# Loads of y inside the last gate, statistics through ScalarE's DMA queue, and joint weights two steps after their loads

## The chip, the cores and the metric

One NeuronCore of a Trainium2 chip. The metric is the device time of one execution in microseconds (us). The kernel before was timed in three runs: median 1971.28 us, from 1967.11 to 1976.27.

## The reference

A trunk of two layers over one sequence of 1024 tokens, width 1024, in float32. In each layer a token mixer's output is gated by a SiLU and projected:

```python
# layer 0: dilated attention, three groups (window, dilation) = (128,1), (512,4), (2048,16), 16 heads each
outs, lses = per group: softmax attention over the window, and its log-denominator
alpha = jax.nn.softmax(jnp.stack(lses, axis=0), axis=0)        # joint weights over the three groups
o = jnp.sum(alpha[..., None] * jnp.stack(outs, axis=0), axis=0)
y = o.reshape(B, S, DIL_WIDTH) * jax.nn.silu(gate)
return y @ w_out
# layer 1: differential attention, 8 heads of two softmaxes, per-head RMSNorm, the same gate and projection
```

Around each mixer stand an RMSNorm before and one after, and the residual.

## The kernel before

**Numbers.** Matmuls run on float32 values split into a high and a low part; a projection is three products (high×high, high×low, low×high). `XH` and `XL`, both resident, are the two parts of the layer's transposed input, 8 tiles of 128 rows called kt 0 to 7. Later the same memory takes the two parts of y, the gated mixer output.

**Layer 0.** Work goes by pairs of heads (`pr` 0 to 7), in a pair by group (`g` 0 to 2), in a unit `(pr, g)` by its two heads `h`. A head has four steps (c = 0 to 3). The main loop (L789 to L828) runs at step i the scores of step i, the transposes of step i − 3 and the products of step i − 5 (`LAG_T`, `LAG_P`). In a step the scores go to PSUM (L603), VectorE masks them and takes the maximum (L610), ScalarE takes the exponential (L613), TensorE transposes (L626), ScalarE and VectorE copy and split the result (`pp`, L630 and L122), TensorE multiplies by v (L653, L665) and ScalarE, VectorE and POOL add up `u` (L671 to L686).

**Filler.** Between these TensorE pieces stand matmuls of the projections: for layer 0 `pqk` (L276: q and k of later units, which are rotated by VectorE and POOL in L248 to L253, stored to `qk_d` by L261 and loaded per head as `qh`, `ql`, `ka` by L268 and L270), then the last gate block (`pg`, also L276, from `late_gates` L311 and `gate_units` L280), then the early part of the output projection (`pe`, L444, in `out_early` L425). The last gate walks kt 0 and 1, then kt 2, 3 up to 7, each for both halves of the tokens, so that a kt's rows of `XH` and `XL` are free once its products are done. After it ScalarE loads the table for the silu (L320), applies it, and loads the exponential's table back.

**Output.** `out_early` loads y of kt 0 to 3 from `y_d` into `XH` and `XL` (`load_y`, L400 to L402, two DMAs of 512 KB per kt), multiplies them with `w_out` (`ow`, `wh`, `wl`, split by L184 and L122 from `raw`, loaded by L421), and stores partial sums (L449, L452). The loads of kt 4 to 6 and the rest follow. Layer 1 uses the same functions; its scores are L951.

**Statistics.** Each head keeps its row maxima and denominators in `st`. `put_stats` (L688) stores them to `st_d`: for g = 0 TensorE transposes them (`tps`, L692), VectorE copies that to `sr` (L694) and four DMAs follow (L699); g = 1 and 2 store `st` directly, four DMAs each (L702, L706). All are of 4 KB. After g = 2 `joint` (L708) loads them as `js` (two DMAs, L712), works out the joint weights on VectorE (L718 to L728) with one exponential on ScalarE (L722), and stores them to `wt_d` (L730). `combine` (L733), a generator of steps run two and four steps later, loads the weights broadcast (`wb`, L753) and the gate (`sil_in`, L763), multiplies on POOL (L759 to L764) and stores y (`y_d`, L384).

**Order.** TensorE's order is set by hand. The order on the other engines and on SP, which issues every DMA, comes from a list scheduler that starts from the order in which the program traces its calls. A DMA, whichever engine issues it, carries one of eight completion semaphores (DMAHW0 to DMAHW7) in turn over the whole program, and the engine that issues it waits until the DMA that carried that semaphore eight places earlier has landed. Each engine runs its instructions in order.

Of the kernel before, what the change touches and what calls it, by code (L numbers as in the profile page):

```python
# [18 lines left out]
P = 128  # L19
# [18 lines left out]
EARLY = 4  # L38
# [54 lines left out]
def trunk(ctx: ExitStack, tc: tile.TileContext, a: dict, out: bass.AP):  # L93
    nc = tc.nc
# [26 lines left out]
    def low(eng, o, full, hi):  # L121
        return eng.tensor_tensor(o, full, hi.bitcast(F32), ALU.subtract)  # L122
# [42 lines left out]
    def ts(j, w=P):  # L165
        return slice(j * w, (j + 1) * w)
# [51 lines left out]
    latest = {}  # L218
# [54 lines left out]
    def project(o, wh, wl, tok, kts=range(KT)):  # L273
        for kt in kts:
            for k, (l, r_) in enumerate(((wh, XH), (wh, XL), (wl, XH))):
                nc.tensor.matmul(o, lhsT=l[:, kt, :], rhs=r_[:, kt, tok],  # L276
                                 start=kt == 0 and k == 0, stop=kt == KT - 1 and k == 2)
                yield 512

    def gate_units(pool, layer, w, fs, eng=None, prepare=None):  # L280

        for f in fs:
            wh, wl = w_tiles([P, KT, P])
            split(wh, wl, load(w[f], [P, KT, P]), eng)
            if prepare and f == fs[-1]:
                prepare()
                banks = [ps.tile([P, 512], F32, tag="pj", name="pg") for _ in range(2)]
                for kts in ((0, 1), *((kt,) for kt in range(2, KT))):
                    for c in range(2):
                        yield from project(banks[c], wh, wl, ts(c, 512), kts)  # L290
                for c in range(2):
                    yield f, c, banks[c]
                return
            for c in range(2):
                o = ps.tile([P, 512], F32, tag="pj", name="pg")
                yield from project(o, wh, wl, ts(c, 512))
                yield f, c, o
# [70 lines left out]
    stored = set()  # L368
# [31 lines left out]
    def load_y(layer, kt):  # L400
        for e, x in enumerate((XH, XL)):
            nc.sync.dma_start(x[:, kt, :].bitcast(F32), y_d[layer][kt, e])  # L402
# [22 lines left out]
    def out_early(pool, layer, w, ws):  # L425

        ws[EARLY - 1] = out_weights(pool, w, EARLY - 1)
        for kt in range(EARLY):
            while (layer, kt) not in stored:
                yield None  # L430
            load_y(layer, kt)
        for n in range(NB):
            if n == NB - HELD:
                while ("heads", layer) not in written:
                    yield None
                for kt in range(EARLY, KT - 1):
                    ws[kt] = out_weights(pool, w, kt)
            parts = []
            for c in range(2):
                bank = ps.tile([P, 512], F32, tag="pj", name="pe")  # L440
                for kt in range(EARLY):
                    wh, wl = ws[kt]
                    for k, (l, r_) in enumerate(((XH, wh), (XH, wl), (XL, wh))):
                        nc.tensor.matmul(  # L444
                            bank, lhsT=l[:, kt, ts(n)], rhs=r_[:, ts(c, 512)],
                            start=kt == 0 and k == 0, stop=kt == EARLY - 1 and k == 2)
                        yield 512
                t = pool.tile([P, 512], F32, tag="t", name="part", bufs=3 - layer)
                nc.scalar.copy(t, bank)  # L449
                parts.append(t)  # L450
            for o, t in zip(partial(n), parts):
                nc.sync.dma_start(o, quarters(t))  # L452
        ws[KT - 1] = out_weights(pool, w, KT - 1)
        banks = ws["banks"] = out_banks(0)
        for kt in range(EARLY, KT - 1):
            while (layer, kt) not in stored:
                yield None
            load_y(layer, kt)
            yield from out_block(0, banks, kt, *ws[kt], kt == EARLY, False)
# [96 lines left out]
    with tc.tile_pool(name="l0", bufs=2) as lp:  # L556
# [4 lines left out]
        class Head:  # L561
# [56 lines left out]
            def transposes(self, c):  # L618

                tp = ps.tile([P, 512], F32, tag="pt", name="tp")  # L620
                n = 0
                for kb in (2 * c, 2 * c + 1):
                    for b in (kb, kb + 1):
                        if (b, kb) in self.pb:
                            self.pt[kb, b] = n
                            nc.tensor.transpose(out=tp[:, ts(n)], in_=self.pb.pop((b, kb)), identity=ident)  # L626
                            n += 1
                w_ = n * P
                pp = lp.tile([P, 2, 512], F32R, tag="pp", name="pp")
                nc.scalar.copy(pp[:, 0, :w_], tp[:, :w_])  # L630
                low(nc.vector, pp[:, 1, :w_], tp[:, :w_], pp[:, 0, :w_])
                self.parts[c] = pp

            def product(self, c):
# [53 lines left out]
        def put_stats(pr, g, st):  # L688

            if g == 0:  # L690
                tp = ps.tile([P, 512], F32, tag="pt", name="tps")
                nc.tensor.transpose(out=tp[:32, :P], in_=st.rearrange("p h e b -> p (h e b)"), identity=ident)  # L692
                sr = lp.tile([32, P], F32, tag="sr", name="sr", bufs=1)
                nc.vector.tensor_copy(sr, tp[:32, :P])  # L694
            for h in range(2):
                for e in range(2):
                    row = st_d[2 * pr + h, g, e]
                    if g == 0:
                        nc.sync.dma_start(  # L699
                            row.rearrange("(b q) -> b q", b=8), sr[16 * h + 8 * e : 16 * h + 8 * e + 8, :])  # L700
                    elif g == 1:
                        nc.sync.dma_start(  # L702
                            row.rearrange("(f q r) -> q f r", f=2, r=4),
                            st[:, h, e, :].rearrange("p (f r) -> p f r", f=2))
                    else:
                        nc.sync.dma_start(row.rearrange("(q r) -> q r", r=8), st[:, h, e, :])  # L706

        def joint(pr):  # L708

            s = lp.tile([P, NG, 2, 16], F32, tag="js", name="js", bufs=1)  # L710
            for h in range(2):
                nc.sync.dma_start(  # L712
                    s[64 * h : 64 * h + 64],
                    st_d[2 * pr + h].rearrange("g e (p i) -> p g e i", i=16))
            m, den = s[:, :, 0, :], s[:, :, 1, :]
            mx = lp.tile([P, 16], F32, tag="jm", name="jm", bufs=1)
            e = lp.tile([P, NG, 16], F32, tag="je", name="je", bufs=1)
            nc.vector.tensor_tensor(mx, m[:, 0, :], m[:, 1, :], ALU.min)  # L718
            nc.vector.tensor_tensor(mx, mx, m[:, 2, :], ALU.min)
            for g in range(NG):  # L720
                nc.vector.tensor_sub(e[:, g, :], mx, m[:, g, :])
            nc.scalar.activation(e, e, AF.Exp)  # L722
            nc.vector.tensor_mul(den, den, e)
            nc.vector.tensor_add(mx, den[:, 0, :], den[:, 1, :])
            nc.vector.tensor_add(mx, mx, den[:, 2, :])
            nc.vector.reciprocal(mx, mx)
            for g in range(NG):
                nc.vector.tensor_mul(e[:, g, :], e[:, g, :], mx)  # L728
            for h in range(2):
                nc.sync.dma_start(  # L730
                    wt_d[2 * pr + h].rearrange("g (p i) -> p g i", i=16), e[64 * h : 64 * h + 64])
# [51 lines left out]
        us, stats, due = {}, {}, {}  # L783
# [5 lines left out]
        for i in range(nst + LAG_P):  # L789
            if i < nst:  # L790
                hd, c = heads[i // 4], i % 4
                if c == 0 and hd.h == 0:
                    stats[hd.pr, hd.g] = lp.tile([P, 2, 2, NB], F32, tag="st", name="st")
                    us[hd.pr, hd.g] = lp.tile([P, T], F32, tag="u", name="u", bufs=4)
                if c == 0:
                    hd.st, hd.u = stats[hd.pr, hd.g][:, hd.h], us[hd.pr, hd.g]
                if c == 1 and i // 4 + 1 < len(heads):
                    nxt = heads[i // 4 + 1]
                    fill.until(NG * nxt.pr + nxt.g)
                    nxt.load()  # L800
                hd.scores(c)
                if i == nst - 1:
                    written.add(("heads", 0))
                fill.at((3 * i + 1) / 24)
                if c == 3 and hd.h == 1 and hd.g == NG - 1:
                    put_stats(hd.pr, hd.g, stats.pop((hd.pr, hd.g)))
                    joint(hd.pr)
            if 0 <= i - LAG_T < nst:
                hd, c = heads[(i - LAG_T) // 4], (i - LAG_T) % 4
                hd.transposes(c)  # L810
# [322 lines left out]
```

## Time and profile before

| what | value |
|---|---|
| timed runs, median of 3 | 1971.28 us |
| profiled execution | 1973.98 us |
| its span, first to last instruction | 1972.1 us |
| mean granted TensorE clock | 0.986 |
| ScalarE, VectorE, POOL busy | 45%, 50%, 40% of the span |
| DMA moved | 397.90 MB, mean 202 GB/s |

The rest of the numbers stand beside the argument below. In the profile PE is TensorE's matmuls, PEld its weight loads, DVE VectorE, ACT ScalarE, POOL GpSimd, and SPq the issue of DMAs on SP. A row of the waits reads: who waited, at which line, for what, us in total, times, longest. A row of the chain of waits or of the timeline begins with the start and the length in us; `out<-in` are the program's names; in brackets stands the idle time ahead and what ended it. In a row of stretches, the stretch is followed by busy times of PE, PEld, DVE, ACT and POOL with their instruction counts, then the granted clock, the DMA engines' busy share and GB/s.

### The profile page before, as it was taken

To read this page: it belongs to the slowest core of one execution; us is meant where nothing else is said; L and a number is where in the kernel's file an instruction comes from. 1 tells how busy PE (TensorE), PEld (TensorE's weight loads), DVE (VectorE), ACT (ScalarE), POOL (GpSimd) and SP (SyncE) were. 2 spreads that over 40 slices of the span, in tenths; PEclk is the share of its full clock that TensorE was granted. 3 is DMA by queue.
4 is the path that set the end of the run, shared out by engine and by line. 5 is a ranking of instruction groups with operands and counts; after the bars stand their busy time and mean duration, and the time that the engine had idled before them with its cause. 6 is when DMAs were issued, how large, how long until landed. Compare 5 with 4: busy or idle time off the path is not lost.

```text
span 1972.1 us, 29075 instructions
## 1 busy us (share of the span) xinstructions
PE 1888.0 (96%) x10008; PEld 1587.9 (81%) x10008; DVE 985.4 (50%) x2618; ACT 885.3 (45%) x2043; POOL 784.2 (40%) x553
## 2 busy tenths in 40 slices
PE   7999999999999999999999878999989899999897
PEld 5788888888888888888888767788878798897786
DVE  5311221135555555555555635550177877778626
ACT  4212112135656565656565555342244455446532
POOL 0000001154585867676776532320742435423011
PEclk9999999999999999999999979999999999999899
DMA  6424344277798989898989798442644565556643
GB/s 225 161 91 133 117 145 155 91 233 219 213 294 239 296 242 283 249 280 259 271 267 267 237 329 217 165 167 87 207 155 132 181 213 182 166 182 196 239 158 128
DMA packets 217539, 397.90 MB, mean 202 GB/s; under 512 B 40880, under 2 KB 123312, under 8 KB 217392
## 3 DMA queue, kind: packets, MB, share of 16 engines
q1 hardware_dynamic: 217392, 396.04, 63.8%
q8 instruction: 80, 1.31, 0.3%
q14 instruction: 67, 0.55, 0.1%
HBM read 254.87 MB, written 132.71 MB: 197 GB/s over the span
## 4 chain that ended last, share of the span: by engine, by line
PE 74%; DMA 10%; DVE 7%; POOL 3%; ACT 3%; issue 2%; SPq 1%; POOLq 0%; ACTq 0%; DVEq 0%
PE pqk L276 29%; PE pv L213 17%; PE pg L276 8%; PE po L391 4%; PE sc L603 3%; PE sc L951 3%; PE pe L444 2%; PE tp L626 2%; PE up L653 2%; PE ob L1004 2%; DMA ql<-qk_d 2%; DMA raw<-in_dil_w_out_dram 1%; DMA qk_d<-r 1%; PE tp L984 1%; DMA wb<-wt_d 1%
## 5 line engine op out<-in xcount | busy, mean ns | idle before, releaser
L276 PE MATMUL pqk<-XL,wh 128*128 128x512 f32 x1024 | 418.7, 409 | 0.0
L276 PE MATMUL pqk<-XH,wh 128*128 128x512 f32 x1024 | 408.3, 399 | 1.7 <-DVE t L252 1.7
L276 PE MATMUL pqk<-XH,wl 128*128 128x512 f32 x1024 | 408.6, 399 | 0.0
L122 POOL TENSOR_TENSOR wl<-raw,wh 128x1024 fp32r<-128x1024 f32 x59 | 141.7, 2401 | 512.3 <-ACT wh L184 509.7
L613 ACT ACTIVATE pm<-pm,st 128x128 f32<-128x128 f32 (+1 forms) x384 | 170.4, 444 | 149.5 <-DVE st L610 148.6
L276 PEld LDWEIGHTS pqk<-XH,wh 128*128 128x128 f32 x1024 | 193.2, 189 | 31.5 <-DVE t L252 3.5
L276 PEld LDWEIGHTS pqk<-XH,wl 128*128 128x128 f32 x1024 | 193.5, 189 | 26.9
L276 PEld LDWEIGHTS pqk<-XL,wh 128*128 128x128 f32 x1024 | 193.1, 189 | 26.9
L122 DVE TENSOR_TENSOR pp<-tp,pp 128x512 fp32r<-128x512 f32 (+2 forms) x192 | 104.3, 543 | 132.5 <-ACT pp L630 131.7
L184 ACT CAST wh<-raw 128x1024 fp32r<-128x1024 f32 x96 | 100.6, 1047 | 144.4 <-PE pqk L276 65.8
L961 ACT ACTIVATE pm<-pm,mx 128x256 f32<-128x256 f32 (+7 forms) x128 | 99.4, 777 | 126.8 <-DVE mx L960 61.1
L213 PE MATMUL pv<-vwh,XH 128*128 128x512 f32 x384 | 153.0, 398 | 2.0 <-ACT XH L158 2.0
L213 PE MATMUL pv<-vwh,XL 128*128 128x512 f32 x384 | 153.0, 398 | 2.0 <-DVE XL L122 1.3
L213 PE MATMUL pv<-vwl,XH 128*128 128x512 f32 x384 | 152.2, 396 | 0.0
L122 DVE TENSOR_TENSOR vs<-pv,vs 128x512 fp32r<-128x512 f32 x64 | 44.2, 690 | 202.2 <-ACT vs L518 194.7
L610 DVE CUSTOM_DVE_ANT_0 pm<-sc,masks 128x128 f32<-128x128 f32 (+1 forms) x384 | 119.1, 345 | 27.2 <-PE sc L603 26.5
L630 ACT CAST pp<-tp 128x512 fp32r<-128x512 f32 (+2 forms) x192 | 89.6, 467 | 80.7 <-PE up L653 62.2
L954 DVE CUSTOM_DVE_ANT_0 pm<-sc,md 128x512 f32<-128x512 f32 (+3 forms) x192 | 102.6, 551 | 38.0 <-PE sc L951 35.5
L122 DVE TENSOR_TENSOR wl<-raw,wh 128x1024 fp32r<-128x1024 f32 x37 | 49.1, 1326 | 137.0 <-ACT wh L184 136.7
L251 POOL TENSOR_TENSOR r<-t 128x512 f32<-128x512 f32 x64 | 84.4, 1319 | 80.2 <-DVE t L250 79.1
L518 ACT CAST vs<-pv 128x512 fp32r<-128x512 f32 x48 | 28.1, 586 | 186.8 <-PE pv L213 186.8
L276 PE MATMUL pg<-XH,wh 128*128 128x512 f32 x256 | 103.1, 403 | 5.0 <-DVE t L252 5.0
(514 smaller groups left out, 4435.4 us busy)
## 6 DMA issues: line engine op xcount, KB each, us to landing
qk_d<-rh SPq DMA_DIRECT2D x64, 512.0 KB
qk_d<-r SPq DMA_DIRECT2D x64, 512.0 KB
qh<-qk_d SPq DMA_DIRECT2D x128, 256.0 KB
ql<-qk_d SPq DMA_DIRECT2D x128, 256.0 KB
ka<-qk_d SPq DMA_DIRECT2D x64, 512.0 KB
v_d<-vs SPq DMA_DIRECT2D x48, 512.0 KB
raw<-in_dil_qk_dram SPq DMA_DIRECT2D x48, 512.0 KB
vt<-v_d SPq DMA_DIRECT2D x48, 512.0 KB
```

What stands on the lines that cost most here:

```text
L122: return eng.tensor_tensor(o, full, hi.bitcast(F32), ALU.subtract)
L184: nc.scalar.copy(wh, raw)
L213: nc.tensor.matmul(o, lhsT=l, rhs=r_, start=first and k == 0, stop=last and k == 3 * KT - 1, skip_group_check=True)
L251: nc.gpsimd.tensor_sub(put(r[0]), nat(t1), nat(t2))
L276: nc.tensor.matmul(o, lhsT=l[:, kt, :], rhs=r_[:, kt, tok], start=kt == 0 and k == 0, stop=kt == KT - 1 and k == 2)
L391: nc.tensor.matmul(banks[c], lhsT=l[:, kt, ts(n)], rhs=r_[:, ts(c, 512)], start=first and k == 0, stop=last and k == 2,)
L603: nc.tensor.matmul(sc[:, cols], lhsT=q[:, ts(b)], rhs=kv, start=k == 0, stop=k == 1)
L610: nc.vector.tensor_tensor_reduce(pm[:, cols], sc[:, cols], m[:, m.shape[1] - w_ :], 1.0, 3.0e38, ALU.add, ALU.min, st[:, 0, j : j + 1])
L613: nc.scalar.activation(pm[:, cols], pm[:, cols], AF.Exp, bias=st[:, 0, j : j + 1], scale=-1.0, accum_out=st[:, 1, j : j + 1])
L630: nc.scalar.copy(pp[:, 0, :w_], tp[:, :w_])
L954: nc.vector.tensor_tensor_reduce(pm[:, k0:k1], sc[:, :w_], m_, 1.0, 3.0e38, ALU.add, ALU.min, mx[:, j : j + 1])
L961: nc.scalar.activation(pm[:, :wq], pm[:, :wq], AF.Exp, bias=mx[:, 0:1], scale=-1.0, accum_out=den)
```

## The change

Three edits. (1) y's loads of kt 0 to 3 are traced inside the last gate, as soon as a kt's gate products are traced, and no longer in `out_early`, where they came after the whole gate. (2) Statistics are stored through ScalarE's queue, 96 DMAs of 4 KB, and the copy to `sr` goes from VectorE to ScalarE, eight times. (3) `joint` stops after its two loads; its arithmetic and its stores run two steps later (one for the last pair), placed behind the latest `low` of a `pp`.

```diff
@@ gate_units
                 for kts in ((0, 1), *((kt,) for kt in range(2, KT))):
                     for c in range(2):
                         yield from project(banks[c], wh, wl, ts(c, 512), kts)
+                    for kt in kts:
+                        if kt < EARLY:
+                            load_y(layer, kt)
@@ out_early
         ws[EARLY - 1] = out_weights(pool, w, EARLY - 1)
-        for kt in range(EARLY):
-            while (layer, kt) not in stored:
-                yield None
-            load_y(layer, kt)
@@ Head.transposes
-                low(nc.vector, pp[:, 1, :w_], tp[:, :w_], pp[:, 0, :w_])
+                latest["low"] = low(nc.vector, pp[:, 1, :w_], tp[:, :w_], pp[:, 0, :w_]).ins
@@ put_stats
-                nc.vector.tensor_copy(sr, tp[:32, :P])
+                nc.scalar.copy(sr, tp[:32, :P])
...
-                        nc.sync.dma_start(
+                        nc.scalar.dma_start(
                             row.rearrange("(b q) -> b q", b=8), sr[16 * h + 8 * e : 16 * h + 8 * e + 8, :])
...
-                        nc.sync.dma_start(
+                        nc.scalar.dma_start(
...
-                        nc.sync.dma_start(row.rearrange("(q r) -> q r", r=8), st[:, h, e, :])
+                        nc.scalar.dma_start(row.rearrange("(q r) -> q r", r=8), st[:, h, e, :])
@@ joint
                     st_d[2 * pr + h].rearrange("g e (p i) -> p g e i", i=16))
+            yield
+
+            with tc.issue_after(latest["low"]):
+                weigh(pr, s)
+
+        def weigh(pr, s):
@@ main loop
-                    joint(hd.pr)
+                    due[i + (2 if hd.pr < 7 else 1)] = job = joint(hd.pr)
+                    next(job)
```

TensorE's order is the same in both. On SP at layer 0's last gate, from the second store of the last unit's rotated half (`qk_d<-r`) on, before:

```order
L261 DMA qk_d<-r 32x4x1024
L753 DMA wb<-wt_d 64x512 x4
L268 DMA qh<-qk_d 64x1024 x2
L268 DMA ql<-qk_d 64x1024 x2
L270 DMA ka<-qk_d 128x1024
L402 DMA XH<-y_d_63 128x1024
L402 DMA XL<-y_d_63 128x1024
L402 DMA XH<-y_d_63 128x1024
L402 DMA XL<-y_d_63 128x1024
L576 DMA vt<-v_d 128x4x128 x2
L402 DMA XH<-y_d_63 128x1024
L402 DMA XL<-y_d_63 128x1024
```

The same place after; the pairs of `XH` and `XL` are kt 1, 2 and 3, and `ka` is that of the next head:

```order
L261 DMA qk_d<-r 32x4x1024
L405 DMA XH<-y_d_63 128x1024
L405 DMA XL<-y_d_63 128x1024
L758 DMA wb<-wt_d 64x512 x4
L405 DMA XH<-y_d_63 128x1024
L405 DMA XL<-y_d_63 128x1024
L405 DMA XH<-y_d_63 128x1024
L405 DMA XL<-y_d_63 128x1024
L268 DMA qh<-qk_d 64x1024 x2
L268 DMA ql<-qk_d 64x1024
L575 DMA vt<-v_d 128x4x128 x2
L268 DMA ql<-qk_d 64x1024
```

Kt 1 has moved ahead of the four `wb`, kt 2 and 3 ahead of the next head's loads; its `ka` is the next row after these.

On ScalarE at the end of the last gate, from the first copy of its result (`sil<-pg`) on, before:

```order
L317 COPY sil<-pg 128x512
L184 CAST wh<-raw 128x1024
L681 COPY ul<-up 64x512
L630 CAST pp<-tp 128x384
L317 COPY sil<-pg 128x512
L320 ACT_TABLE_LOAD
L320 ACTIVATE sil<-sil 128x1024
L613 ACT_TABLE_LOAD
```

And after, with the semaphores that a row waits for; the earlier DMAs that carry DMAHW4, 6, 0 and 2 here are XL of kt 4, the w_out tile of kt 4, a `wb`, and the first `y_d<-u`:

```order
L320 COPY sil<-pg 128x512 [waits PE_49]
L184 CAST wh<-raw 128x1024 [waits DMAHW2_49,PE_49]
L693 COPY sr<-tps 32x128 [waits PE_49]
L680 COPY ul<-up 64x512 [waits PE_49,Activation_49]
L629 CAST pp<-tp 128x384 [waits PE_49]
L320 COPY sil<-pg 128x512 [waits PE_49]
L698 DMA st_d<-sr 8x128 [waits DMAHW4_49,Activation_49]
L698 DMA st_d<-sr 8x128 [waits DMAHW6_49]
L698 DMA st_d<-sr 8x128 [waits DMAHW0_49]
L698 DMA st_d<-sr 8x128 [waits DMAHW2_49]
L323 ACT_TABLE_LOAD
L323 ACTIVATE sil<-sil 128x1024 [waits Activation_49]
```

The `sr` copy and pair 7's four stores stand between the second copy and the table load. In the other pairs the four stores stand behind a `pp`, and the last one's turn falls behind `sil_in`.

On SP at layer 1's last gate, from the w_out tile on, before:

```order
L421 DMA raw<-in_diff_w_out_dram 128x1024 [waits DMAHW2_49,DVE_49]
L268 DMA qh<-qk_d 64x1024 [waits DMAHW3_49,PE_49]
L268 DMA qh<-qk_d 64x1024 [waits DMAHW4_49]
L268 DMA ql<-qk_d 64x1024 [waits DMAHW5_49,PE_49]
L268 DMA ql<-qk_d 64x1024 [waits DMAHW6_49]
L384 DMA y_d_64<-sq 128x512 [waits DMAHW7_49,Activation_49]
L384 DMA y_d_64<-os__17548 128x512 [waits DMAHW0_49,DVE_49]
L270 DMA ka<-qk_d 128x1024 [waits DMAHW1_49]
```

And after, where DMAHW1 was XH of kt 0 in the last row above and DMAHW5 is XL of kt 1 here:

```order
L424 DMA raw<-in_diff_w_out_dram 128x1024 [waits DMAHW2_49,DVE_49]
L268 DMA qh<-qk_d 64x1024 [waits DMAHW3_49,PE_49]
L405 DMA XH<-y_d_64 128x1024 [waits DMAHW4_49,PE_49]
L405 DMA XL<-y_d_64 128x1024 [waits DMAHW5_49]
L268 DMA qh<-qk_d 64x1024 [waits DMAHW6_49]
L387 DMA y_d_64<-sq 128x512 [waits DMAHW7_49,Activation_49]
L405 DMA XH<-y_d_64 128x1024 [waits DMAHW0_49,PE_49]
L387 DMA y_d_64<-os__17548 128x512 [waits DMAHW1_49,DVE_49]
L405 DMA XL<-y_d_64 128x1024 [waits DMAHW2_49]
L268 DMA ql<-qk_d 64x1024 [waits DMAHW3_49]
L268 DMA ql<-qk_d 64x1024 [waits DMAHW4_49]
L270 DMA ka<-qk_d 128x1024 [waits DMAHW5_49]
```

Kt 1 and kt 2 have moved ahead of `ka`. Elsewhere on SP the head loads qh, qh, ql, ql of a pair's first unit now stand ahead of the two stores of the joint weights (`wt_d`), and `ka` behind them. On VectorE the eight `sr` copies are gone, and L718 to L728 stand later: of pair 6, behind the last rotation `t L252` and one `pp`, with the scores' L610 between its lines.

## The prediction

> **What bounds the kernel now.** The page comes first. TensorE is busy 96% of the span, so the change can only move what is left, 1972.1 − 1888.0 = 84 us, and the clock after a wait.
>
> ```profile
> span 1972.1 us, 29075 instructions
> PE 1888.0 (96%) x10008; PEld 1587.9 (81%) x10008; DVE 985.4 (50%) x2618; ACT 885.3 (45%) x2043; POOL 784.2 (40%) x553
> ```
>
> The view by stretches says where those 84 us lie (first the length and TensorE's busy time, near the end of a row the granted clock, the DMA engines' share, GB/s).
>
> ```profile
> 420.00:760.00 340.00, 340.00 (x1910) 290.03 (x1909) 185.06 (x596) 195.24 (x538) 222.62 (x152) 1.00 0.83 251
> 760.00:1100.00 340.00, 338.45 (x1908) 288.36 (x1908) 190.95 (x613) 199.37 (x559) 238.49 (x167) 1.00 0.90 267
> 1100.00:1180.00 80.00, 61.27 (x302) 50.41 (x301) 34.77 (x107) 41.49 (x107) 33.79 (x26) 0.83 0.90 287
> 1820.00:1840.00 20.00, 12.95 (x64) 10.77 (x63) 7.40 (x25) 5.08 (x13) 1.24 (x2) 0.74 1.04 368
> ```
>
> In layer 0's attention (420 to 1100) TensorE loses 1.55 us of 680: whatever the change takes off another engine there is hidden already. At layer 0's last gate it loses 80 − 61.27 = 18.7 us, beside clock. At layer 1's last gate it loses 7.05 us. The waits name them:
>
> ```profile
> PE sc L951 <- DMA ka<-qk_d: 7.8, 2, 6.7
> PE pe L444 <- DMA XH<-y_d: 6.1, 3, 4.4
> PE sc L603 <- DMA st_d<-st: 5.1, 1, 5.1
> PE pg L276 <- DVE t L252: 5.0, 1, 5.0
> PE tp L626 <- DVE pp L122: 2.3, 1, 2.3
> ```
>
> Rows two to five are the 18.5 us of layer 0's last gate. The third is put down to `st_d` because it landed last; the score was waiting for its head's qh, ql and ka, which SP issued just ahead of that store (`ka` below at 1170.69, the score at 1176.27). The chain of waits through this stretch shows that from 1122 to 1157 each link is a transfer that waited for an earlier one:
>
> ```profile
> 1101.92 2.32 DMA js<-st_d
> ...
> 1121.97 9.33 DMA raw<-in_dil_w_out_dram
> 1131.36 9.36 DMA qk_d<-r
> 1140.74 7.39 DMA ql<-qk_d
> 1148.15 8.64 DMA XH<-y_d
> 1156.92 0.77 PE pe L444
> ```
>
> **The body, 420 to 1100.** Gone from VectorE: eight copies of 0.28 us, and the waits of the joint weights for their loads, 19.4 us in all.
>
> ```profile
> DVE jm L718 <- DMA js<-st_d: 19.4, 8, 4.7
> POOL u L759 <- DMA wb<-wt_d: 26.1, 13, 17.4
> L694 DVE COPY sr<-tps x8: 278/279/279, 467.2 to 1144.0; 32x128 f32<-32x128 f32 x8
> 757.46 0.33 SPq L763 DMA_DIRECT2D sil_in<-sil_d  x1
> 755.01 0.48 ACT L630 CAST pp<-tp 128x384 fp32r<-128x384 f32 x1
> 757.97 0.40 ACT L613 ACTIVATE pm<-pm,st 128x128 f32<-128x128 f32 x1 [2.48 <-DVE st L610]
> ```
>
> TensorE waited for none of this there, so the gain is nothing. ScalarE gets the 96 stores (0.33 us each, as an estimate from the issue of `sil_in` below: 32 us over 680, beside 394.6 busy) and stays at 63%. What is new is that its in-order stream now waits where SP's did. A store takes its turn of eight completion semaphores; of a pair's four `sr` stores the last waits until `sil_in` has landed. In the quoted pair ScalarE is through with its cast at 755.5, `sil_in` is issued at 757.46, and the next ScalarE work starts at 757.97. A load that takes 2 to 9 us to land (2.32 and 9.36 are the ends in the chain above) holds ScalarE to 760 or 767, 2 to 9 us later than it started. A step is 4.0 us (the copies of L694 are 24 steps a pair and 676.8 / 7 = 96.7 us apart); scores, transposes and products lie 3 and 2 steps apart, so by an estimate one step, 4 us, of lateness is free. Between +0 and +8 for all pairs; I take +1, because these loads come in the middle of a 0.83 to 0.90 share and not of 1.04.
>
> The weights go out about a step (4 us) later, and `wb` with them. POOL waited 26.1 us for `wb` in all, and TensorE for none of that between 420 and 1100: nothing, with POOL's slack as the cover; if it goes, up to the same 4 us a pair. Pair 7's weights, one step later, cost TensorE less than the 2.3 us of the last row of waits: between −2 and +4, I take 0.
>
> **Layer 0's last gate up to the score at 1157.** Two things move. First, the joint of pair 6 held VectorE (first row: the stretch in which the DMA engines had room):
>
> ```profile
> 1105.00:1110.00 5.00, 4.83 (x27) 4.12 (x27) 4.86 (x19) 2.78 (x8) 2.05 (x2) 1.00 0.23 69
> 1104.34 0.17 DVE L718 TENSOR_TENSOR jm<-js 128x16 f32<-128x16 f32 x1 [4.74 <-DMA js<-st_d]
> 1120.61 0.79 PE L276 MATMUL pg<-XH,wh 128*128 128x512 f32 x1 [4.97 <-DVE t L252]
> 1136.52 0.63 PE L276 MATMUL pg<-XH,wl 128*128 128x512 f32 x1
> 1140.34 0.39 PE L276 MATMUL pg<-XH,wl 128*128 128x512 f32 x1
> ```
>
> VectorE's lateness, 4.74 us, is TensorE's wait of 4.97 a step or two on. In the new order `t L252` and a `pp` stand ahead of L718, but the load still lands at 1101.92 + 2.32 = 1104.24, and with it L718 in the new order too, so I count half of the wait as gone, 2.5 us. Second, kt 1's loads of y go ahead of four `wb`, and kt 2 and 3 ahead of the next head's qh, ql, vt and ka. That takes the 6.1 us of waits in `pe` away; but `ka` now stands last (it waits for kt 3's half to land), and the score behind those products wants it. With the same bytes through DMA engines at a share above 1, `ka` lands about when kt 3 did, 1156.92, and the 6.1 us come back as one wait of the score. What is left is a head start: qh, qh, ql, ql (four of 256 KB) go out ahead of the joint weights, in 1105 to 1110, where a quarter of the DMA time (0.23) was used; 1 MB at 368 GB/s is 2.8 us. One step goes the other way: the `ow` cast comes ahead of two exponentials and a copy on ScalarE, about 2 us at the 2.3 us wait. I take −2, with −8 (all of 4.97 and the 2.8) and +4 as ends.
>
> **From 1157 to layer 0's last head.** Here the stores meet the largest transfers.
>
> ```profile
> 1146.25 0.59 ACT L317 COPY sil<-pg 128x512 f32<-128x512 f32 x1
> 1146.86 1.28 ACT L320 ACT_TABLE_LOAD   x1
> 1148.15 1.06 ACT L320 ACTIVATE sil<-sil 128x1024 f32<-128x1024 f32 x1
> 1154.63 0.48 ACT L630 CAST pp<-tp 128x384 fp32r<-128x384 f32 x1 [3.12 <-PE up L653]
> 1155.57 1.70 SPq L753 DMA_DIRECT2D wb<-wt_d  x2
> 1163.63 0.35 SPq L384 DMA_DIRECT2D y_d<-u  x1
> 1170.69 0.58 SPq L270 DMA_DIRECT2D ka<-qk_d  x1
> 1162.82 0.49 PE L626 MATMUL tp<-ident,pm 128*128 128x128 f32 x3
> 1176.27 0.45 PE L603 MATMUL sc<-ka,qh 128*128 128x128 f32 x1 [5.11 <-DMA st_d<-st]
> ```
>
> ScalarE now issues pair 7's four `sr` stores between the copy at 1146.25 and the table load. The four wait for the landing of XL kt 4, the w_out tile of kt 4, a `wb`, and the first `y_d<-u`; that last one SP issues behind `ka` and `wb`. Its issue is near 1157.5 (the two `wb` end at 1157.27, POOL no longer holds it), its landing 7.4 us on by the `ql` of the chain, which has its size: ScalarE is free at about 1165, not at 1146.84. Behind the stores are two table loads of 1.28 and the silu, 1.06 (3.6 us), two exponentials (0.4 each for the smaller form above, 0.9 as an estimate), and the cast that was at 1154.63 and frees the bank of the transpose at 1162.82, 0.5 and, estimated, as much for VectorE's half: 1165 + 3.6 + 0.9 + 1.0 = 1170.5. Against 1162.82 TensorE stands for 7.7 us there. From there to the score at 1176.27 it has 1171.2 − 1162.8 = 8.4 us of work (the 5.11 us of that row taken off), and about 2 us for the clock behind the stall: 1180.9, 4.6 us later. The 5.11 us are covered by then (its `ka` still lands about 1176), and the clock that was low behind that wait, 1 us or so, is saved: +4. These are times of the before; the −2 above moves all of them alike. The ends: −5 if the stores clear before 1157 (then only SP's lighter load counts, and 5.11 goes), +10 if the second pair of stores, behind qh and ka of the next head, holds ScalarE again before the bank copies.
>
> The Trainium skill, "DMA: Bandwidth & Descriptors", section "Issuing engines are not separate DMA queues", says that issuing from several engines only saves the time in which a sequencer starts a DMA. By that, the sum for this edit would be 96 issues off SP, none on TensorE's path, and the terms +1 and +4 both 0: 1973. The trace agrees in that the DMA share, not SP's 0.33 us, is what fills this stretch. The same page, "Anatomy of one DMA", says that a semaphore wait is held on the issuing sequencer; no run here shows it yet for ScalarE.
>
> On the clock: after the 2.33 us wait at 1132.5 the matmul of 0.39 us became one of 0.63 (the rows at 1136.52 and 1140.34), for about 4 us. I charge 2 us behind each stall.
>
> **Layer 1's last gate.**
>
> ```profile
> 1817.20 7.46 DMA XH<-y_d
> 1824.68 8.70 DMA ka<-qk_d
> ```
>
> Before, SP's `ka` waits for XH of kt 0 to land, and lands 8.70 us on. After, kt 1 and kt 2 stand ahead of it and it waits for XL of kt 1. It need not wait for kt 2 to land, so I count kt 1 and half of kt 2 in front of it, 3 × 512 KB: at 368 GB/s 4.2 us. TensorE waits for that score already, so all of it is on the path; the products of y gain nothing, since all three waits of `pe` are layer 0's. +4, ends 0 (the transfers overlap, and `ka` lands when it did) and +7 (another landing of 7.46 in full).
>
> **Sum.** +1 − 2 + 4 + 4 = +7 us. The profiled execution took 1973.98 us (span 1972.1 and 1.9 around it), so it would take 1981; the three timed runs have a median of 1971.28, 2.7 lower, so I forecast 1978. A difference under 0.5% (9.9 us) is about what a measurement of this kernel can't tell from none.
>
> **Rivals.** *ScalarE is late in the body too* (slower): the hold behind `sil_in` passes the free 4 us in each pair. At the long end, a landing of 9.36 us less the 4.5 that are free there (757.97 + 4 − 757.46), one pair would cost 4.9; if three of seven do, +14 more: 1992. For it: a DMA share of 0.83 to 0.90, and landings of 9 us where it is 1.04. Against it: ScalarE idles 2.48 us at that place anyway, and TensorE has run through VectorE's waits of up to 4.7 us (the 19.4 in all cost it 5). It decides from the point where `sil_in` takes over 4.5 us to land.
>
> *The last gate is freed* (faster): pair 6's wait goes in full (−5), y's products and the score run through (−6), `st_d` is out of g2's way, and layer 1's `ka` lands as before: −12 of the 18.5, 1959. For it: all four rows of waits are touched by the edits. Against it: the chain of transfers through 1157 has the same bytes.
>
> *It only changes seats* (no change): y's loads swap with `ka`, ScalarE's hold lies beside a stall that is there anyway, layer 1 is overlapped: 1972. The rule of the Trainium skill on issuing engines, above, leads near to this.
>
> **How the numbers follow.** Forecast 0.45, slower rival 0.20, faster rival 0.20, no change 0.15. Of the forecast, whose own range is 1968 to 1988, two thirds lie within 0.5% (below 1981.1) and one third above. Within: 0.30 + 0.15 + 0.02 + 0.02 of the two rivals' inner ends = 0.49; slower 0.15 + 0.18 = 0.33; faster 0.18. The range goes to both rivals, 1959 to 1992.
>
> **What would show it.** In the new profile: DVE's wait at L718 shrunk; `pe` with no wait on y at 1145 to 1157 and a wait of `sc` on `ka` in its place; ScalarE idle for over 10 us ahead of L320's table load, released by a DMA; TensorE waiting in `tp` for a `pp`; the wait of `sc L951` on `ka` grown from 6.7 to about 11. Wrong would be: ScalarE's table load within 5 us of the second copy, layer 1's wait unchanged, or new TensorE waits between 420 and 1100.

## The result, and the profile after

The changed kernel took 1986.09 us (median of 4 runs, 1983.41 to 1989.68) beside 1970.37 us for the kernel before in the same job: ratio 1.0074, 95% interval 1.0051 to 1.0098. It is slower, by 10 to 19 us, most likely about 15. The forecast was 1978.

The profiled execution of the new kernel is its fastest run (1983.41 us), and that of the kernel before one of its slower ones (1973.98), so the two profiles are 9.4 us apart and show only that much of the 15. Page of the new kernel, and its stretches:

```profile
span 1981.4 us, 29006 instructions
PE 1882.8 (95%) x10008; PEld 1583.2 (80%) x10008; DVE 976.7 (49%) x2610; ACT 885.9 (45%) x2051; POOL 783.8 (40%) x553
```

```profile
420.00:760.00 340.00, 339.63 (x1906) 289.63 (x1905) 182.16 (x590) 195.03 (x537) 222.04 (x151) 1.00 0.84 251
760.00:1100.00 340.00, 335.54 (x1893) 286.05 (x1893) 185.83 (x603) 197.12 (x555) 237.67 (x166) 1.00 0.89 266
1100.00:1180.00 80.00, 54.30 (x275) 44.45 (x274) 30.34 (x96) 37.10 (x96) 35.79 (x28) 0.82 0.93 281
```

TensorE loses 4.8 us of the attention body where it lost 1.55, and 25.7 us of layer 0's last gate where it lost 18.7. Its waits after (compare the five rows of before):

```profile
PE sc L957 <- DMA ka<-qk_d: 15.2, 2, 13.4
...
PE sc L602 <- DMA ka<-qk_d: 9.7, 1, 9.7
PE tp L625 <- DVE pp L122: 8.8, 2, 7.7
PE pqk L276 <- DVE t L252: 4.8, 4, 2.0
...
PE pg L276 <- DVE t L252: 3.3, 1, 3.3
PE pe L443 <- DMA XH<-y_d: 3.0, 2, 2.0
```

Three of the old waits have shrunk: `pg` from 5.0 to 3.3, `pe` from 6.1 to 3.0, and the 5.1 us ahead of the last unit are gone. Three have come: the score on `ka` in layer 0 (9.7), the transpose on a `pp` (7.7), and layer 1's score on `ka`, 13.4 in place of 6.7.

TensorE's order is the same in both kernels, so the same matmul can be looked up in both timelines. Its start after, less its start before:

| TensorE instruction (start before) | later by, us |
|---|---|
| body at 400 | 1.2 |
| body at 1059, behind its waits for `t L252` | 4.5 |
| `pe` at 1151, behind the last gate | −5.5 |
| score on `ka` at 1157.49 | 4.5 |
| transpose at 1162.82 | 14.1 |
| first score of the last unit, 1176.27 | 11.2 |
| output product at 1239.9 | 5.0 |
| layer 1, score at 1808 | 2.8 |
| layer 1, score on `ka` at 1833.42 | 9.5 |

The score on `ka` takes back the 5.5 us that `pe` had gained and leaves TensorE as late as it was ahead of the gate. Two other steps are large: the transpose (+10), most of it given back by 1240, and layer 1's score (+7). The chain of waits of the new kernel through layer 0's last gate shows the first, link by link (start, length, what):

```profile
1142.59 8.87 DMA XH<-y_d
1151.47 10.45 DMA ka<-qk_d
1161.99 9.00 DMA y_d<-u
1171.30 1.28 ACT L323
...
1176.35 0.57 DVE pp L122
1176.96 0.90 PE tp L625 x3
```

A load of y lands; then SP may issue `ka`; `ka` lands; then SP may issue the store of y; that lands; then ScalarE may issue its last store, and behind that come its table loads, the silu, the exponentials and the cast that TensorE waits for. ScalarE's timeline, where the DMA row merges the four stores (the first at 1164.55, the last at 1171.00):

```profile
1146.34 0.59 ACT L320 COPY sil<-pg 128x512 f32<-128x512 f32 x1
1164.55 6.73 ACTq L698 DMA_DIRECT2D st_d<-sr  x4
1171.30 1.28 ACT L323 ACT_TABLE_LOAD   x1 [24.37 <-DMA st_d<-sr]
```

ScalarE does nothing for 24.4 us with work in its stream. The chain of waits at layer 1's last gate:

```profile
1822.60 9.55 DMA XL<-y_d
1832.16 10.65 DMA ka<-qk_d
1842.91 0.66 PE sc L957 x2
```

Before, `ka` went out 7.5 us after the load of XH kt 0 (1817.20 to 1824.68) and landed in 8.70. Now it goes out 12.1 us after that load (issued at 1820.02), since XL of kt 1 must land first, and takes 10.65: 4.7 and 2.0 us, the 6.7 us by which the wait has grown.

### The profile page after: what moved, and what is told of

It is laid out like the page before. It is cut to its first block, busy times and chain, and to the rows that moved or that the text cites. A ratio compares the mean times of both kernels' runs of the same rounds, so it can differ in the third digit from the quotient of the medians.

```text
span 1981.4 us, 29006 instructions
## 1 busy us (share of the span) xinstructions
PE 1882.8 (95%) x10008; PEld 1583.2 (80%) x10008; DVE 976.7 (49%) x2610; ACT 885.9 (45%) x2051; POOL 783.8 (40%) x553
## 5 line engine op out<-in xcount | busy, mean ns | idle before, releaser
L122 POOL TENSOR_TENSOR r<-r,rh 128x1024 fp32r<-128x1024 f32 x44 | 105.3, 2402 | 4.7 <-ACT rh L257 4.7
```

## The experiments

My theory after the result: three separate losses, ScalarE's hold at layer 0's last gate, `ka` behind y's loads in layer 1, and the waits for `t L252` in the body. The rival: y's loads going ahead of `ka` cost it in both layers, and ScalarE's hold only lies in the shadow of that. Each kernel was timed in five rounds against the kernel before on the same chip; the kernel before had medians of 1973.1 to 1975.8 us in these jobs, so 0.001 of a ratio is 2 us.

**Edit 1 alone.**

```diff
 gate_units:   +for kt in kts: if kt < EARLY: load_y(layer, kt)
 out_early:    -for kt in range(EARLY): ... load_y(layer, kt)
```

> Only edit 1 (y's loads traced inside the last gate); statistics on SP and the joint as before. Theory A (three separate losses: ScalarE held by its stores at layer 0's last gate, ka of layer 1 behind y's loads, rotation waits in the body): layer 1's wait of the score on ka stays grown (12 to 14 us against 6.7), layer 0's last gate costs 0 to +3, together +6 to +10 us. Rival B (all of it comes from y's loads going ahead of ka in both layers; ScalarE's hold only lies in the shadow of that wait): +13 to +17 us.

Measured 1.0043 (1.0024 to 1.0061), +8.5 us. Its waits:

```profile
PE sc L950 <- DMA XH<-y_d: 13.3, 1, 13.3
...
PE sc L602 <- DMA XL<-y_d: 9.0, 1, 9.0
```

The two scores wait as in the full change (the row names the transfer that landed last). In the timelines TensorE is 3.0 us later than before at the first score of the last unit, and 6.7 at layer 1's score on `ka`. The rival's 13 us are not there.

**Edit 2 alone.**

```diff
 put_stats:    -nc.vector.tensor_copy(sr, ...)   +nc.scalar.copy(sr, ...)
               -nc.sync.dma_start(...)           +nc.scalar.dma_start(...)   (three places)
```

> Only edit 2 (statistics through ScalarE, sr copied by ScalarE). Theory A: ScalarE stands over 15 us ahead of the silu's table load at layer 0's last gate, TensorE waits in tp for a pp, +3 to +8 us; layer 1 unchanged. Rival B: within +-3 us, with the hold in the shadow of other waits. If the waits for t L252 between 420 and 1100 (1.55 us before, 4.8 after) come from this edit they are here, +3 us of the sum.

Measured 1.0021 (1.0007 to 1.0034), +4 us. TensorE's waits for the cast in layer 0, 11.4 us the longest, and ScalarE's in the same stretch:

```profile
PE tp L626 <- DVE pp L122: 14.2, 2, 11.4
```

```profile
ACT L320 <- DMA st_d<-sr: 20.3, 1, 20.3
```

The hold is there without any load of y moved, so it isn't a shadow of edit 1. Of the 11.4 us, 6.7 are left at the last unit's score (the old wait of 5.1 is covered) and 2.8 at 1211.

**Edit 3 alone.**

```diff
 joint:        two loads, then  +yield  +with tc.issue_after(latest["low"]): weigh(pr, s)
 main loop:    -joint(hd.pr)   +due[i + (2 if hd.pr < 7 else 1)] = job = joint(hd.pr); next(job)
```

> Only edit 3 (joint's arithmetic two steps after its loads). Theory A: VectorE's wait at L718 gone or small, TensorE's wait of 4.97 us for t L252 at 1115 smaller by 2 to 3 us; time -4 to 0. Rival B: the same, since nothing in it touches ka. If the body's waits for t L252 come from this edit they are here, and the sum is 0 to +3.

Measured 0.9984 (0.9972 to 0.9997): 3 us faster. The wait for `t L252` at 1115 went from 5.0 to 3.8:

```profile
PE pg L276 <- DVE t L252: 3.8, 1, 3.8
PE pqk L276 <- DVE t L252: 3.0, 3, 1.3
```

In its timeline TensorE is level with before at 1109, 5.3 us ahead at 1140 and 4.6 ahead at 1240. It is the one edit of the three that helps.

**Edits 1 and 3**, statistics as before.

```diff
 the full change without its edit in put_stats
```

> Edits 1 and 3, statistics as before on SP with VectorE's copy: the change without its second edit. Theory A: faster than the full change by what ScalarE's stores cost, 5 to 9 us, so +7 to +11 against before. Rival B: like the full change, +13 to +17.

Measured 1.0042 (1.0023 to 1.0060), +8 us: the first theory's number, though more than the +8.5 and −3 of the two edits alone would give; the intervals cover that gap.

**Edit 1 in layer 0 alone.**

```diff
 gate_units:   +if kt < EARLY and layer == 0: load_y(layer, kt)
 out_early:    for kt in (range(EARLY) if layer else ()): ...
```

> Edit 1 in layer 0 alone; layer 1 loads y as before, edits 2 and 3 left out. Theory A: of the +8.5 us of edit 1, layer 1's wait on ka is 6.6; here that wait is 6 to 8 us again as before, and the time is -1 to +4 against before. Rival: the loss is made in layer 0, where the score waits 9 us for its loads in place of 6.1 us in pe; then still +6 to +9.

Measured 1.0007 (0.9988 to 1.0027). Waits for `ka`, layer 0 and layer 1:

```profile
PE sc L606 <- DMA ka<-qk_d: 14.8, 2, 9.6
...
PE sc L954 <- DMA ka<-qk_d: 7.1, 2, 6.3
```

Layer 1's wait is 6.3 us again, and with it the loss is gone. In layer 0 the waits for y have turned into a longer one for `ka`, 9.6 us in place of 6.1 (the second of the row, 5.2, is the last unit's, 5.1 before): the swap of seats. In its timeline that isn't free: TensorE goes from 1.6 us ahead at 1100 to 2.5 late at the score on `ka`. But at 1850, behind layer 1's wait, it is level with before, and no cost shows in the time.

**Edit 2 for pairs 0 to 6**, pair 7 on SP as before.

```diff
 put_stats:    +dma = nc.sync if pr == 7 else nc.scalar      (and VectorE's copy for pr 7)
```

> Edit 2 for pairs 0 to 6; pair 7's twelve stores stay on SP and its copy on VectorE. Theory A (the hold of ScalarE at the last gate is all that edit 2 costs): no wait of 11 us in tp, ScalarE's idle time ahead of L320's table load under 2 us, time -2 to +2. Rival (ScalarE's stores cost in the body, pair by pair): as with the whole edit, +3 to +6, with waits for t L252 of 3 us or more between 420 and 1100.

Measured 1.0005 (0.9990 to 1.0021): seven pairs of eight on ScalarE's queue cost nothing that shows, though the waits for `t L252` are 4.5 us here, as the rival would have it:

```profile
PE pqk L276 <- DVE t L252: 4.5, 5, 1.7
```

So what edit 2 costs I put down to pair 7, though the intervals of the two kernels (1.0007 to 1.0034 and 0.9990 to 1.0021) overlap.

**The full change with both places undone.**

```diff
 edits 1 (layer 0 alone), 2 (pairs 0 to 6) and 3 together
```

> The full change, but pair 7's statistics on SP with VectorE's copy, and layer 1's loads of y as before. Theory A: of the full change's +15 us the hold (5 to 8) and layer 1 (6.6) are gone: -2 to +4 against before. Rival (the three edits together disturb the body and the last gate beyond these two places): +6 or more.

Measured 1.0008 (0.9993 to 1.0023): not to be told from before. ScalarE's table load follows the copy at once, and layer 1 waits as before:

```profile
1144.86 0.59 ACT L320 COPY sil<-pg 128x512 f32<-128x512 f32 x1
1145.47 1.28 ACT L323 ACT_TABLE_LOAD   x1
```

```profile
PE sc L966 <- DMA ka<-qk_d: 6.7, 1, 6.7
```

**The full change with one place undone**, first layer 1's loads, then pair 7's stores.

```diff
 as the kernel above, but pair 7 on ScalarE again
 as the kernel above, but layer 1's loads inside its last gate again
```

> The full change, with layer 1's loads of y as before. Theory A: layer 1's wait of the score on ka goes from 13.4 back to 6 to 7.5 us, ScalarE still stands over 20 us at layer 0's last gate; +5 to +10 against before. Rival (the hold and layer 1 are not additive, layer 1's loss is in part a shift that the tail absorbs): within 3 us of the full change, +11 to +16.

> The full change, with pair 7's statistics on SP and its copy on VectorE. Theory A: no wait of TensorE in tp for a pp at 1160 to 1180 and ScalarE's idle time ahead of the table load under 2 us, layer 1's wait still 12 to 14 us: +5 to +10 against before. Rival: +11 to +16.

Measured 1.0030 (1.0013 to 1.0046) with layer 1 as before, and 1.0054 (1.0035 to 1.0072) with pair 7 on SP. The second is +10.7 us, a little past the +5 to +10 that I had expected and short of the rival's +11.

```profile
PE tp L629 <- DVE pp L122: 11.9, 2, 7.7
...
PE sc L961 <- DMA XH<-y_d: 7.5, 1, 7.5
```

```profile
PE sc L962 <- DMA XH<-y_d: 13.4, 1, 13.4
```

Each kernel keeps the one wait and has lost the other (the first two rows, then the last). The ledger from both ends: layer 1 is 1.0074 − 1.0030 or 1.0054 − 1.0008, about 0.0045 or 9 us; pair 7 is 1.0074 − 1.0054 or 1.0030 − 1.0008, about 0.0021 or 4 us; 0.0008 is left. Each difference is uncertain by some 5 us, so layer 1's are clear of zero and pair 7's are not; edit 2 alone and without pair 7 (1.0021 and 1.0005) put the same place at 3. That pair 7's stores cost time rests on edit 2 alone, whose interval is clear of zero, and on the waits that come and go with them.

**Half a dose in layer 1**: y of kt 0 and 1 inside the gate, nothing else.

```diff
 gate_units:   +if kt < 2 and layer == 1: load_y(layer, kt)
 out_early:    for kt in range(2 if layer else 0, EARLY): ...
```

> Layer 1 alone, half a dose: y of kt 0 and 1 inside the last gate, kt 2 and 3 as before; layer 0, statistics and joint as before. In the new order only kt 1 stands ahead of ka, and ka's turn waits for a qh issued before kt 1, not for kt 1's own XL. If what ka waits for is the landing of kt 1 (its turn), the wait of sc on ka is 7 to 9 us, near the 6.7 of before, and the time +0 to +3. If it is the bytes that stand ahead of ka (1 MB of kt 1 of the 1.5 MB that count in the change), the wait is 10 to 12 us and the time +3 to +6.

Measured 1.0005 (0.9988 to 1.0022). The wait, the score in TensorE's timeline, and SP's timeline:

```profile
PE sc L954 <- DMA ka<-qk_d: 8.6, 1, 8.6
```

```profile
1833.47 0.48 PE L954 MATMUL sc<-ka,qh 128*128 128x128 f32 x1 [8.64 <-DMA ka<-qk_d]
```

```profile
1815.37 0.92 SPq L405 DMA_DIRECT2D XH<-y_d  x1
...
1818.12 0.42 SPq L405 DMA_DIRECT2D XL<-y_d  x1
...
1825.39 0.32 SPq L270 DMA_DIRECT2D ka<-qk_d  x1
```

Here `ka` goes out 10.0 us after XH of kt 0, between 7.5 before and 12.1 with all of it, 7.3 us after XL of kt 1. Two thirds of the bytes that I had counted in front of it give 1.9 of the 6.7 us, as expected if the turn decides and less than the bytes would have it.

**y of kt 0 and 1 in layer 0, and edit 3.**

```diff
 gate_units:   +if kt < 2 and layer == 0: load_y(layer, kt)
 out_early:    for kt in range(0 if layer else 2, EARLY): ...     (and edit 3)
```

> Edit 3, and y's loads inside layer 0's last gate for kt 0 and 1 alone; kt 2 and 3, layer 1 and the statistics as before, so that ka stays ahead of kt 2 and 3. If the order of the transfers behind the gate decides (theory A): pe's wait of 4.4 us for kt 1 gone without a new wait for ka, -3 to -8 us against before. Rival (the DMA engines are full there and any load moved forward moves another back): as edit 3 alone, -3 us or slightly worse.

Measured 0.9989 (0.9973 to 1.0004), no better than edit 3 alone.

```profile
PE pe L447 <- DMA XH<-y_d: 8.7, 2, 7.2
...
PE sc L606 <- DMA ka<-qk_d: 5.7, 1, 5.7
```

The load that was moved forward moved another back: 7.2 us for a later kt, where the longest wait for y was 4.4 before. The 5.7 us for `ka` are the last unit's, 5.1 before. The rival was right.

**Edit 3, and `ka` ahead of y in layer 1**, the reverse of edit 1.

```diff
 heads_in:     latest["ka"] = nc.sync.dma_start(ka ...).ins
 out_early:    if layer: with tc.issue_after(latest["ka"]): load_y(layer, kt)      (and edit 3)
```

> Edit 3, and the opposite of edit 1 in layer 1: all of y's loads there are placed behind the last head's ka on SP; layer 0 and the statistics as before. If the turn and the bytes ahead of ka are what the score waits for (theory A): the wait of sc on ka near 1830, 6.7 us before, goes to 0 to 2, the products of y wait under 2 us, and the time is -6 to -11 against before. Rival (ka is held by something else, such as qh and ql or the stores of y): the wait stays over 4 us and the time is that of edit 3 alone, -3.

Measured 0.9976 (0.9960 to 0.9993): faster than the kernel before, by 5 us. The wait:

```profile
1835.88 0.45 PE L962 MATMUL sc<-ka,qh 128*128 128x128 f32 x1 [4.83 <-DMA ka<-qk_d]
```

I had expected a wait of 0 to 2; over 4 is what the rival gave, by which something else than y holds `ka`. `ka` goes out at 1825.60 here, behind the same qh, ql and a store of y, 5.5 us before TensorE is ready for the score, and before it was 2.0. So its turn came 3.4 us earlier, but its landing took 10.3 us in place of 8.70 with nothing of y ahead of it, and only 1.9 of the 6.7 us went. What this adds to edit 3 alone can't be told: the intervals overlap.

## Why the prediction was right or wrong

**The direction and the range held; the size didn't.** +7 us was forecast as most likely, with 0.49 on no change within 0.5% and 0.33 on slower than that; it was +15, in the forecast's upper third and toward the slower rival. One of the signs of being wrong that I had named came true, new waits of TensorE between 420 and 1100. The two profiles show 9.4 of the 15 us, so what the terms cost beyond that rests on the ratios.

**The body, +1.** TensorE's waits there went from 1.5 us (the row is the kernel before, 80 to 1100) to 4.8, +3.

```profile
PE pqk L276 <- DVE t L252: 1.5, 2, 1.2
```

The mechanism of the slower rival is there: ScalarE waits behind `sr` and `sil_in` six times in 80 to 1100,

```profile
ACT pm L612 <- DMA st_d<-sr: 13.6, 4, 5.3
ACT pm L612 <- DMA sil_in<-sil_d: 9.3, 2, 6.1
```

and with 6.1 us at most it passes the 4 us that I had counted as free. But with pairs 0 to 6 alone the time didn't move beyond its interval (1.0005, up to 1.0021). Why TensorE waits more for `t L252` stays open: the runs with the joint but not the statistics moved have 3.0 to 7.7 us of it, those with the statistics alone 3.2 and 4.5, those with y's loads alone 1.0 to 1.7. So edits 2 and 3 each bring it, and it isn't shown how.

**Layer 0's last gate, −2.** In the timelines 4.5 us late before it and 4.5 behind it: nothing. In the profiles of single edits two effects cancel from 1100 to the score on `ka`: edit 3 alone gains 3.9 us there, edit 1 alone loses 3.8. Right in its parts: the wait for `t L252` shrank (by 1.7 us, 2.5 counted), `pe`'s waits came back as one of the score on `ka` (9.7 us), and `ka` landed when kt 3 did, shift allowed for. The head start failed: the four loads went out at 1110.5 to 1112.9, later than the 1105 I had in mind, since their buffers come free with a score of TensorE, for which SP stood 4.8 us.

**The hold, +4.** Right in kind and place, and about 4 us in the two differences of runs, neither of them clear of zero. I had put ScalarE's release at 1165; it was 1171.30. The store of y went out at 1161.99 and not near 1157.5, since its turn waited for `ka`, which took 10.45 us to land; and it took 9.00 itself, where I had taken 7.4. TensorE's lateness at the last unit rose by 6.7 us, and by 1240 it was given back: 5.0 late against 4.5 ahead of the hold in the profile. There the price hangs on which waits of the tail it covers.

**Layer 1, +4: the step that failed.** "It need not wait for kt 2 to land, so I count kt 1 and half of kt 2 in front of it" sized the term by bytes. The runs put it at 6.7 us in the profile and some 9 in time, uncertain by 5. `ka` waited for a turn, the whole landing of XL of kt 1 (9.55 us from an issue that came late itself): 4.7 of the 6.7. The other 2.0 are its own landing, 10.65 us in place of 8.70, and why that was longer stays open. The end that I gave, +7 for another landing in full, was the better value.

**The rivals.** The last gate wasn't freed: the seats were swapped there, as the third rival had it. The rule of the Trainium skill by which only issue time is saved ("DMA: Bandwidth & Descriptors", "Issuing engines are not separate DMA queues") would have given zero for edit 2; pairs 0 to 6 agree with it (1.0005), pair 7 doesn't (about 0.0021 of the time, by the differences above). The same page of the Trainium skill says ("Anatomy of one DMA — SWDGE (gpsimd) path") that a wait for a semaphore is held on the issuing sequencer. The trace agrees with that for ScalarE: the 24.37 us ahead of L323.

## What to carry to other kernels

Before a DMA moves to the queue of an engine that computes, look at which landing its turn waits for: the 4 KB store costs 0.3 us to issue, and its place in the stream cost 24 us of ScalarE where the large transfers pass. Loads that are moved ahead of others in a stretch where the DMA engines are full take their time from those others, and it is worth nothing unless TensorE wants the moved one first. Price a load that falls behind another by the landing that its turn waits for, not by the bytes between them.

## What the runs showed of the hardware

A 4 KB store issued from ScalarE landed as slowly as one from SP: 5.43 us in the new kernel (the row below, at pair 6's last store), 5.46 at the same place before.

```profile
1099.60 5.43 DMA st_d<-st
```

The landing of the same 512 KB of layer 1's `ka` varied with the order, but not with the bytes ahead of it alone. With the old order there it took 8.70 us in the kernel before and 9.0 to 9.5 in three others (edit 3 alone, edit 1 in layer 0 alone, both places undone). With kt 1 and 2 ahead it took 10.65 in the full change and 10.0 with edits 1 and 3. With kt 1 alone ahead it took 8.1, from issue to score, and with no y ahead 10.3. Why is open.
